# Attention of a hybrid mLSTM / windowed-attention layer: scores kept in PSUM through maximum, two exponentials and low half, outputs normalised at the end, heads spread over an iteration

## The chip, the cores and the metric

The kernel runs on one core of a Trainium2 chip. The metric is the device time of one execution in microseconds. Everything below that is a time comes from the profile of one execution of the kernel before, from its three timed runs, or from an answer of its trace.

## The reference

One layer: modulated RMS norm, one combined input projection, two token mixers side by side (a bidirectional mLSTM and windowed grouped-query attention), a gated merge, and a convolutional feed-forward. The change touches only attention of the latent tokens. Sizes: 1024 latent tokens, 256 context tokens, 16 query heads in 4 groups over 4 key heads, head size 64, window 128 in blocks of 128.

```python
def one_block(args):
    blk, qblk, kblk, vblk = args
    ...
    s_lat = jnp.einsum('btkgd,bskd->bkgts', qblk, kblk).astype(jnp.float32) * ATT_SCALE
    s_lat = jnp.where(valid, s_lat, NEG_INF)
    s_ctx = jnp.einsum('btkgd,bskd->bkgts', qblk, k_ctx).astype(jnp.float32) * ATT_SCALE
    p = jax.nn.softmax(jnp.concatenate([s_lat, s_ctx, sink_b], axis=-1), axis=-1).astype(v.dtype)
    return (jnp.einsum('bkgts,bskd->btkgd', p[..., :3 * T], vblk)
            + jnp.einsum('bkgts,bskd->btkgd', p[..., 3 * T:3 * T + C], v_ctx))
```

So each block of 128 queries of one group sees up to three key tiles of its band, two context tiles and one sink logit a head: five key tiles, or four at the two ends of the sequence.

## The kernel before

Matrix products run in fp32r, and an operand that must be exact is split in two, a high part and the rest, so that a product becomes two or three. Attention is a software pipeline over 32 pairs (g, b): group g of four heads, block b of 128 queries. Iteration n of the loop at L764 does, for different pairs at once:

- `proj` (L551): 24 products of the projected queries, key and value of pair n (tile `pq`), and from them V, the sums of squares `ss` and the rotated queries and key `qf`, on ACT, DVE and POOL;
- `stacks` (L593) for pair n-1: the key scaled and doubled (`kf`, on DVE), three transposes on TensorE (tile `qt`), then queries `QT` and keys `KA`, `KB` as high part and rest;
- `filler` (L725): 24 products of a later gate (tile `g`), which need nothing of attention and are dealt out among the others;
- `scores` (L619) for pair n-3: for each of four heads four products into a PSUM tile `s` of two banks (two such tiles), DVE's masked maximum (L645), which also copies the scaled scores to SBUF (`P`), ACT's exponential with the sum (L649); after all four heads one short chain with the sink (L653 to L657) gives four reciprocals; then for each head POOL multiplies to an f16 high half (L663), DVE makes the f16 low half (L664, `scalar_tensor_tensor`), and SP issues a DMA transpose of both halves into `T` (L665);
- `pv` (L672) for pair n-4: for each key tile ACT widens the high half of T to fp32r (`ph`) and POOL the low half (`pl`), TensorE multiplies both with V into `po`, and ACT, DVE and SP bring out `o` to DRAM.

One buffer holds T, three each hold `ph` and `pl`, six hold P. A scheduler of the language orders the program: each engine's queue is in order, and it may place an instruction ahead of one written earlier; `tc.issue_after` pins some. SP's queue carries, besides the transposes, the loads of weights (`w1r`, `fr`, `wmb`) and the stores (`sga`, `sgm`, `attT`). The modulation products (`mod_product`) put one or two sums (`macc`) a turn on DVE.

Of the kernel before, what the change touches and what calls it, by code (L numbers as in the profile page):

```python
# [36 lines left out]
PSCALE = 32768.0  # L37
# [496 lines left out]
def stage_attention(E, st, at):  # L534
# [13 lines left out]
    G = {}  # L548
    S1, S2, S3, S4 = {}, {}, {}, {}

    def proj(g, b):  # L551
        if b == 0:
# [5 lines left out]
            )  # L558
        n = f"{g}_{b}"
        ps = mm_tile(f"pq{n}")  # L560
        wn = 400 if g == 0 else 384
        mm3(nc, ps[:, :wn], hT, G[g]["w"], sl(b * P, P), sl(0, wn))
# [29 lines left out]

    def stacks(g, b):  # L593
# [3 lines left out]
        nc.vector.tensor_scalar(kf, qf[:, None, 256:320].to_broadcast([P, 2, HD]), ss[:, 4:5], None, op0=ALU.mult)  # L597


# [3 lines left out]
        nc.tensor.transpose(pt[:, 256:384], kf.rearrange("p r d -> p (r d)"), ident)  # L603
        QT = wp.tile([P, 512], F32R, tag="QT", name=f"QT{n}", bufs=3)
# [14 lines left out]
    def scores(g, b):  # L619
# [12 lines left out]
        Ps, prior = [], None  # L632
        for h in range(4):
            ps = s_tile(f"s{n}_{h}")
            q = QT[:, h * P : (h + 1) * P]
            with behind(prior):
                nc.tensor.matmul(ps[:, lat], q, KA[:, b0 * P : b1 * P], start=True, stop=False)  # L637
                nc.tensor.matmul(ps[:, lat], q, KB[:, b0 * P : b1 * P], start=False, stop=True)
                nc.tensor.matmul(ps[:, con], q, KcA[:, g], start=True, stop=False)
                last = nc.tensor.matmul(ps[:, con], q, KcB[:, g], start=False, stop=True)  # L640
            prior = FILL.products(6) if h in (0, 1, 2) else None
            pm = pp.tile([P, 960], F32, tag="P", name=f"P{n}_{h}", bufs=6)
            ex = pm[:, W // 2 : W // 2 + W]
            hh = 4 * g + h
            nc.vector.tensor_tensor_reduce(  # L645
                ex, ps[:, every], mask, scale=ss[:, h : h + 1], scalar=nsink[:, hh : hh + 1],
                op0=ALU.add, op1=ALU.min, accum_out=st4[:, h : h + 1],
            )
            nc.scalar.activation(  # L649
                ex, ex, AF.Exp, bias=st4[:, h : h + 1], scale=-1.0, accum_out=st4[:, 4 + h : 5 + h]  # L650
            )
            Ps.append((ex, pm.bitcast(F16)[:, : 2 * W].rearrange("p (a c) -> p a c", a=2)))
        nc.vector.tensor_tensor(st4[:, 8:12], st4[:, 0:4], sink[:, 4 * g : 4 * g + 4], op=ALU.add)  # L653
        nc.scalar.activation(st4[:, 8:12], st4[:, 8:12], AF.Exp)
        nc.vector.tensor_tensor(st4[:, 8:12], st4[:, 8:12], st4[:, 4:8], op=ALU.add)
        nc.vector.tensor_scalar(st4[:, 8:12], st4[:, 8:12], 1.0 / PSCALE, None, op0=ALU.mult)
        nc.vector.reciprocal(st4[:, 12:16], st4[:, 8:12])  # L657
        nk = W // P
        T = tq.tile([P, 5120], F16, tag="T", name=f"T{n}")[:, : nk * 1024].rearrange("p (a k h q) -> p a k h q", a=2, h=4, q=P)
        for h in range(4):  # L660
            ex, (hi, lo) = Ps[h][0], (Ps[h][1][:, i] for i in range(2))
            r = st4[:, 12 + h : 13 + h]
            nc.gpsimd.tensor_scalar(hi, ex, r, 1.0, op0=ALU.mult, op1=ALU.mult)  # L663
            nc.vector.scalar_tensor_tensor(lo, ex, r, hi, op0=ALU.mult, op1=ALU.subtract)  # L664
            nc.sync.dma_start_transpose(  # L665
                T.rearrange("p a k h q -> p (a k) h q")[:, :, h], Ps[h][1].rearrange("p a c -> p (a c)")
            )
# [96 lines left out]
    for n in range(N + 5):  # L764
# [3 lines left out]
        if n < N:  # L768
            proj(*seq[n])
# [1297 lines left out]
```

## Time and profile before

| | |
|---|---|
| median of 3 runs | 1987.13 us (1987.01 to 1990.43) |
| profiled execution | 1987.95 us, span 1986.1 us, granted clock 0.98 |
| attention's steady part, 148 to 696 us | 548 us |

In the profile, PE is TensorE, PEld its weight loads, DVE VectorE, ACT ScalarE, POOL GpSimd, SP the engine that issues most DMAs. A row of a group reads: line, engine, operation, output<-inputs, shapes, count, then busy us and mean ns of one, then the idle time just before them and what ended it. A row of waits reads: who waited <- for whom, us in all, times, longest. A row of the timeline reads: start, duration, engine, line, operation, count of merged instructions, and in brackets the idle time ahead of it and what ended it. In the table of windows each engine has busy time and count.

### The profile page before, as it was taken

Reading aid. Unit: us, or ns where it says so; the run is one execution under the profiler, and the core shown is the slowest. Engines: PE = TensorE matmul, PEld = TensorE weight load, DVE = VectorE, ACT = ScalarE, POOL = GpSimd, SP = SyncE. Lnnn points to the kernel's source line nnn. Section 1 sums busy time; section 2 is a strip of 40 time slices with the busy share of each in tenths; the row PEclk is TensorE's granted clock in tenths of the full one; section 3 lists DMA queues with packets and bytes.
Section 4 is the critical chain, followed back from the end, with each engine's and each line's share of the span. In section 5 each row is a group of like instructions: output and inputs, shape, how many; then the busy total and the mean of one; then the engine's idle time right before and its main releaser. Section 6 shows DMA issues by size and latency. Waiting matters only on the chain.

```text
span 1986.1 us, 27108 instructions
## 1 busy us (share of the span) xinstructions
PE 1856.4 (93%) x9029; PEld 1563.1 (79%) x9029; DVE 1513.0 (76%) x2928; ACT 982.5 (49%) x1942; POOL 440.6 (22%) x676
## 2 busy tenths in 40 slices
PE   7998888888898789999999999999999999999999
PEld 4887677677787578988788888787888888888887
DVE  3867877878888748584857788769988988997565
ACT  4635555455555525444444566347544444455441
POOL 1225555455555514030202002100000000000000
PEclk9999998899999999999999999999999999999999
DMA  9636755756666652524351994642255544489851
GB/s 350 189 110 121 151 126 118 161 115 135 151 139 131 141 156 64 178 65 158 121 168 39 368 380 151 210 156 74 106 202 194 187 170 162 177 294 335 314 181 64
DMA packets 299165, 338.17 MB, mean 170 GB/s; under 512 B 175232, under 2 KB 199696, under 8 KB 296208
## 3 DMA queue, kind: packets, MB, share of 16 engines
q1 hardware_dynamic: 284624, 310.21, 51.2%
q10 hardware_dynamic: 14400, 26.22, 4.0%
q8 instruction: 71, 1.16, 0.3%
q14 instruction: 70, 0.57, 0.1%
HBM read 220.42 MB, written 76.10 MB: 149 GB/s over the span
## 4 chain that ended last, share of the span: by engine, by line
PE 47%; DVE 3%; DMA 2%; issue 2%; ACT 2%; POOL 1%; POOLq 0%; ACTq 0%; DVEq 0%
PE pa L1645 4%; PE pa L1646 4%; PE pa L1647 4%; PE dx L1647 2%; PE dx L1645 2%; PE dx L1646 2%; PE pb L1646 2%; PE pb L1647 2%; PE pb L1645 2%; PE yb L1645 2%; PE yb L1646 2%; PE yb L1647 2%; PE dy L1647 2%; PE dy L1646 2%; PE dy L1645 2%
## 5 line engine op out<-in xcount | busy, mean ns | idle before, releaser
L664 DVE SCALAR_TENSOR_TENSOR P<-P,st 128x640 f16<-128x640 f32 (+1 forms) x128 | 151.0, 1237 | 26.5 <-POOL P L663 26.1
L663 POOL TENSOR_SCALAR P<-P,st 128x640 f16<-128x640 f32 (+1 forms) x128 | 134.0, 1062 | 76.9 <-DVE st L657 72.1
L645 DVE CUSTOM_DVE_ANT_0 P<-s,maskA,nsink 128x640 f32<-128x640 f32 (+1 forms) x128 | 113.7, 906 | 22.3 <-PE s L640 20.1
L691 POOL TENSOR_SCALAR pl<-T 128x512 fp32r<-128x512 f16 x152 | 100.9, 682 | 89.1 <-DMA T<-P 74.4
L649 ACT ACTIVATE P<-P,st 128x640 f32<-128x640 f32 (+1 forms) x128 | 101.6, 795 | 35.4 <-DVE st L645 33.0
L46 ACT ACTIVATE ph<-T 128x512 fp32r<-128x512 f16 x152 | 86.9, 619 | 59.6 <-DMA T<-P 54.0
L742 PE MATMUL g<-hH,fh 128*128 128x512 f32 x256 | 103.7, 405 | 2.2 <-ACT fo L46 2.2
L742 PE MATMUL g<-hH,fl 128*128 128x512 f32 x256 | 102.1, 399 | 0.0
L742 PE MATMUL g<-hL,fh 128*128 128x512 f32 x256 | 102.0, 398 | 0.0
L99 PE MATMUL pq<-w1l,hH 128*128 128x384 f32 (+1 forms) x256 | 89.9, 351 | 11.0 <-DVE w1l L76 11.0
L98 PE MATMUL pq<-w1h,hH 128*128 128x384 f32 (+1 forms) x256 | 89.2, 348 | 1.4 <-ACT w1h L46 1.4
L1059 POOL TENSOR_SCALAR kwh<-k,gcall 128x128 fp32r<-128x128 f32 x72 | 34.7, 486 | 248.4 <-PE dC L99 202.6
L100 PE MATMUL pq<-w1h,hL 128*128 128x384 f32 (+1 forms) x256 | 88.8, 347 | 0.0
L98 PE MATMUL kv<-w1h,hH 128*128 128x384 f32 x208 | 71.1, 343 | 4.6 <-ACT w1h L46 2.9
L99 PE MATMUL kv<-w1l,hH 128*128 128x384 f32 x208 | 71.3, 343 | 0.6 <-DVE w1l L76 0.6
L100 PE MATMUL kv<-w1h,hL 128*128 128x384 f32 x208 | 70.4, 339 | 0.0
L637 PE MATMUL s<-KA,QT 128*128 128x384 f32 (+1 forms) x128 | 47.4, 371 | 24.6 <-DVE st L645 24.5
L1783 ACT ACTIVATE cv<-ua,vecT 128x1024 f32<-128x1024 f32 x22 | 27.4, 1244 | 84.0 <-DVE ua L1756 84.0
L1645 PE MATMUL dx<-dwh,dfh 128*128 128x512 f32 (+1 forms) x176 | 68.4, 388 | 0.0
L1647 PE MATMUL dx<-dwh,dfl 128*128 128x512 f32 (+1 forms) x176 | 68.3, 388 | 0.0
L1646 PE MATMUL dx<-dwl,dfh 128*128 128x512 f32 (+1 forms) x176 | 68.2, 387 | 0.0
L683 PE MATMUL po<-ph,V 128*128 128x512 f32 x88 | 41.9, 476 | 24.2 <-ACT ph L46 23.9
(602 smaller groups left out, 6297.4 us busy)
## 6 DMA issues: line engine op xcount, KB each, us to landing
ur<-in_w_up SPq DMA_DIRECT2D x22, 1024.0 KB, 4.9
wmb<-in_w_modB SPq DMA_DIRECT2D x48, 256.0 KB, 3.0
f_d<-cv SPq DMA_DIRECT2D x22, 512.0 KB, 2.7
wm<-in_w_modA SPq DMA_DIRECT2D x16, 512.0 KB, 10.2
fr<-in_w_g SPq DMA_DIRECT2D x32, 256.0 KB, 3.0
drf<-fs_d SPq DMA_DIRECT2D x15, 512.0 KB, 7.4
drw<-wt_d SPq DMA_DIRECT2D x14, 512.0 KB, 6.5
w1b<-in_w_cx SPq DMA_DIRECT2D x16, 388.0 KB, 4.6
```

The source lines that it names most:

```text
L98: nc.tensor.matmul(ps, lh[:, ls], rh[:, rs], start=start and i == 0, stop=False)
L99: nc.tensor.matmul(ps, lh[:, ls], rl[:, rs], start=False, stop=False)
L100: nc.tensor.matmul(ps, ll[:, ls], rh[:, rs], start=False, stop=stop and i == n - 1)
L645: nc.vector.tensor_tensor_reduce(ex, ps[:, every], mask, scale=ss[:, h : h + 1], scalar=nsink[:, hh : hh + 1], op0=ALU.add, op1=ALU.min, a ...
L649: nc.scalar.activation(ex, ex, AF.Exp, bias=st4[:, h : h + 1], scale=-1.0, accum_out=st4[:, 4 + h : 5 + h])
L663: nc.gpsimd.tensor_scalar(hi, ex, r, 1.0, op0=ALU.mult, op1=ALU.mult)
L664: nc.vector.scalar_tensor_tensor(lo, ex, r, hi, op0=ALU.mult, op1=ALU.subtract)
L691: nc.gpsimd.tensor_scalar(plo, lo, 1.0 / PSCALE, 1.0, op0=ALU.mult, op1=ALU.mult)
L742: return lambda: nc.tensor.matmul(ps, w, x, start=i == 0, stop=i == len(todo) - 1)
L1645: nc.tensor.matmul(ps, lh, rh, start=start and i == 0, stop=False, skip_group_check=True)
L1646: nc.tensor.matmul(ps, lh, rl, start=False, stop=False, skip_group_check=True)
L1647: nc.tensor.matmul(ps, ll, rh, start=False, stop=stop and i == n - 1, skip_group_check=True)
```

## The change

Scores stay in the PSUM tile. DVE's masked maximum writes back to it. ACT adds a constant (15 ln 2, for the scale of the f16 halves) to the maximum, makes the f16 high half by one exponential straight from PSUM, and by a second exponential, in place in PSUM, the f32 value with the sum. DVE's low half is a `tensor_tensor` of the PSUM value and the f16 half. The transpose of a head stands directly behind its low half and no longer behind the reciprocals. The halves are not normalised: the four reciprocals of a pair are transposed to a row on TensorE (`norm_row`), go through DRAM and come back broadcast to 64 partitions (`R`), and POOL multiplies the finished output with them. POOL now widens both halves of T, by a copy, for all key tiles of a pair at the head of an iteration; `kf` is made by ACT. The loop is written so that the four heads of a pair, the 24 projection products, the 24 filler products and the ten value products alternate in fixed pieces. Buffers of T, `ph`, `pl` and `s` stay as many; P has four.

```diff
+    def norm_row(pt):
+        if not SUMS:
+            return
+        sums, j = SUMS.pop()
+        nc.tensor.transpose(pt, sums, ident)
+        row = wp.tile([4, P], F32, tag="row", name=f"row{j}", bufs=1)
+        copy_act(nc, row, pt)
+        nc.sync.dma_start(norm_d[j].rearrange("(h t) -> h t", h=4), row)
+        R[j] = wp.tile([HD, 512], F32, tag="R", name=f"R{j}", bufs=1)
+        nc.sync.dma_start(R[j], norm_d[j : j + 1].to_broadcast([HD, 512]))
...
     def stacks(g, b):
...
-        nc.vector.tensor_scalar(kf, qf[:, None, 256:320].to_broadcast([P, 2, HD]), ss[:, 4:5], None, op0=ALU.mult)
+        copy_act(nc, kf, qf[:, None, 256:320].to_broadcast([P, 2, HD]), scale=ss[:, 4:5])
...
+        norm_row(pt[0:4, 384:512])
...
+        def head(h, prior=None):
+            s = s_tile(f"s{n}_{h}")
...
+            e = s[:, every]
             hh = 4 * g + h
             nc.vector.tensor_tensor_reduce(
-                ex, ps[:, every], mask, scale=ss[:, h : h + 1], scalar=nsink[:, hh : hh + 1],
-                op0=ALU.add, op1=ALU.min, accum_out=st4[:, h : h + 1],
+                e, e, mask, scale=ss[:, h : h + 1], scalar=nsink[:, hh : hh + 1],
+                op0=ALU.add, op1=ALU.min, accum_out=st4[:, 8 + h : 9 + h],
             )
-            nc.scalar.activation(
-                ex, ex, AF.Exp, bias=st4[:, h : h + 1], scale=-1.0, accum_out=st4[:, 4 + h : 5 + h]
-            )
...
-        for h in range(4):
-            ex, (hi, lo) = Ps[h][0], (Ps[h][1][:, i] for i in range(2))
-            r = st4[:, 12 + h : 13 + h]
-            nc.gpsimd.tensor_scalar(hi, ex, r, 1.0, op0=ALU.mult, op1=ALU.mult)
-            nc.vector.scalar_tensor_tensor(lo, ex, r, hi, op0=ALU.mult, op1=ALU.subtract)
-            nc.sync.dma_start_transpose(
-                T.rearrange("p a k h q -> p (a k) h q")[:, :, h], Ps[h][1].rearrange("p a c -> p (a c)")
-            )
+            m = st4[:, h : h + 1]
+            nc.scalar.activation(m, st4[:, 8 + h : 9 + h], AF.Identity, bias=shift)
+            two = pp.tile([P, 1280], F16, tag="P", name=f"P{n}_{h}", bufs=4)
+            hi, lo = two[:, :W], two[:, W : 2 * W]
+            nc.scalar.activation(hi, e, AF.Exp, bias=m, scale=-1.0)
+            nc.scalar.activation(e, e, AF.Exp, bias=m, scale=-1.0, accum_out=st4[:, 4 + h : 5 + h])
+            nc.vector.tensor_tensor(lo, e, hi, op=ALU.subtract)
+            nc.sync.dma_start_transpose(T[:, :, h], two[:, : 2 * W])
...
-            copy_act(nc, ph, hi, scale=1.0 / PSCALE)
-            nc.gpsimd.tensor_scalar(plo, lo, 1.0 / PSCALE, 1.0, op0=ALU.mult, op1=ALU.mult)
+            for i, x in enumerate((ph, plo)):
+                nc.gpsimd.tensor_copy(x, T[:, i * nk + kb].rearrange("p h q -> p (h q)"))
...
+        def end():
+            o2 = wp.tile([HD, 512], F32, tag="o2", name=f"o2{n}", bufs=1)
+            copy_act(nc, o2, po[HD:P])
+            nc.vector.tensor_tensor(o2, po[0:HD], o2, op=ALU.add)
+            nc.gpsimd.tensor_tensor(o2, o2, R.pop(g * NB + b), op=ALU.mult)
...
     for n in range(N + 5):
...
+        if head:
+            head(0)
+        if turned:
+            stacks(*turned)
+        elif SUMS:
+            norm_row(tp_tile(f"nr{n}")[0:4, :P])
+        last = new.some(17)
+        if head:
+            head(1, last)
+        new.some(7)
+        if now:
+            projected(*now, ps)
+        last = FILL.some(6)
+        if head:
+            head(2, last)
+        FILL.some(9)
+        last = old.some(4)
+        if head:
+            head(3, last)
+            sums()
+        for k in (2, 2, 2):
+            FILL.some(3)
+            old.some(k)
+        if end:
+            end()
```

How the scheduled queues move is shown at three places, all in the iteration that scores group 1, block 3 (`P1_3_0` to `P1_3_3` are its heads). First ACT, around the last exponentials of the block. Before:

```order
L46 ACTIVATE ph1_2_1_3472<-T1_2_3269 128x512
L649 ACTIVATE P1_3_0_3410,st1_3_3398<-P1_3_0_3410,st1_3_3398 128x640
L649 ACTIVATE P1_3_1_3424,st1_3_3398<-P1_3_1_3424,st1_3_3398 128x640
L649 ACTIVATE P1_3_2_3438,st1_3_3398<-P1_3_2_3438,st1_3_3398 128x640
L46 ACTIVATE ph1_2_2_3476<-T1_2_3269 128x512
L46 ACTIVATE ph1_2_3_3482<-T1_2_3269 128x512
L649 ACTIVATE P1_3_3_3446,st1_3_3398<-P1_3_3_3446,st1_3_3398 128x640
L654 ACTIVATE st1_3_3398<-st1_3_3398 128x4
L46 ACTIVATE ph1_2_4_3488<-T1_2_3269 128x512
L46 ACTIVATE fo6_0_3508<-g6_0_3397 128x512
```

The change:

```order
L688 ACTIVATE st1_3_3449<-st1_3_3449,shift_1111 128x1
L691 ACTIVATE P1_3_2_3570<-s1_3_2_3563,st1_3_3449 128x640
L692 ACTIVATE s1_3_2_3563,st1_3_3449<-s1_3_2_3563,st1_3_3449 128x640
L46 ACTIVATE kf1_6_3670<-qf1_6_3548,ss1_6_3543 128x128
L46 ACTIVATE fo6_0_3624<-g6_0_3447 128x512
L688 ACTIVATE st1_3_3449<-st1_3_3449,shift_1111 128x1
L46 ACTIVATE o21_2_3619<-po1_2_3451 64x512
L691 ACTIVATE P1_3_3_3595<-s1_3_3_3588,st1_3_3449 128x640
L692 ACTIVATE s1_3_3_3588,st1_3_3449<-s1_3_3_3588,st1_3_3449 128x640
L698 ACTIVATE st1_3_3449<-st1_3_3449 128x4
```

The widening copies `ph` are gone from between the exponentials; `kf`, `fo` and `o2` of other pairs now stand between those of the third head and those of the fourth.

Second POOL, around the copies of T for the pair before (`T1_2`). Before:

```order
L573 TENSOR_TENSOR ss1_6_3358<-ss1_6_3358,expo_62 128x5
L574 TENSOR_SCALAR ss1_6_3358<-ss1_6_3358 128x4
L590 TENSOR_TENSOR qf1_6_3363<-qf1_6_3363,t21_6_3364 128x320
L691 TENSOR_SCALAR pl1_2_0_3469<-T1_2_3269 128x512
L691 TENSOR_SCALAR pl1_2_1_3473<-T1_2_3269 128x512
L691 TENSOR_SCALAR pl1_2_2_3477<-T1_2_3269 128x512
L691 TENSOR_SCALAR pl1_2_3_3483<-T1_2_3269 128x512
L691 TENSOR_SCALAR pl1_2_4_3489<-T1_2_3269 128x512
L663 TENSOR_SCALAR P1_3_0_3410<-P1_3_0_3410,st1_3_3398 128x640
```

The change:

```order
L718 CAST pl1_2_2_3461<-T1_2_3255 128x512
L600 TENSOR_SCALAR ss1_6_3543<-ss1_6_3543 128x5
L718 CAST ph1_2_3_3464<-T1_2_3255 128x512
L718 CAST pl1_2_3_3465<-T1_2_3255 128x512
L718 CAST ph1_2_4_3468<-T1_2_3255 128x512
L718 CAST pl1_2_4_3469<-T1_2_3255 128x512
L601 TENSOR_TENSOR ss1_6_3543<-ss1_6_3543,expo_62 128x5
L602 TENSOR_SCALAR ss1_6_3543<-ss1_6_3543 128x4
L618 TENSOR_TENSOR qf1_6_3548<-qf1_6_3548,t21_6_3549 128x320
L728 TENSOR_TENSOR o21_2_3619<-o21_2_3619,R10_3494 64x512
L718 CAST ph1_3_0_3638<-T1_3_3450 128x512
```

`qf` of pair (1, 6), which `kf1_6` above reads, stood ahead of the copies of T and now stands behind all ten of them.

Third SP. Before:

```order
L756 DMA sga_d_66<-fo6_0_3508 128x512
L665 DMA_TRANSPOSE T1_3_3454<-P1_3_0_3410 128x10x128
L665 DMA_TRANSPOSE T1_3_3454<-P1_3_1_3424 128x10x128
L665 DMA_TRANSPOSE T1_3_3454<-P1_3_2_3438 128x10x128
L665 DMA_TRANSPOSE T1_3_3454<-P1_3_3_3446 128x10x128
L700 DMA attT_d_64<-o21_2_3504 64x4x128
```

The change:

```order
L628 DMA norm_d_1110<-row10_3491 4x128
L221 DMA wmb22_3628<-in_w_modB 128x512
L750 DMA fr7_1_3830<-in_w_g 128x512
L73 DMA w1r33_3835<-in_w_att 128x2x384
L630 DMA R10_3494<-norm_d_1110 64x512
L694 DMA_TRANSPOSE T1_3_3450<-P1_3_0_3479 128x10x128
L694 DMA_TRANSPOSE T1_3_3450<-P1_3_1_3527 128x10x128
L694 DMA_TRANSPOSE T1_3_3450<-P1_3_2_3570 128x10x128
L772 DMA sga_d_66<-fo6_0_3624 128x512
L221 DMA wmb23_3631<-in_w_modB 128x512
L729 DMA attT_d_64<-o21_2_3619 64x4x128
L694 DMA_TRANSPOSE T1_3_3450<-P1_3_3_3595 128x10x128
```

The two DMAs of the reciprocals stand ahead of the block's first transpose, and a store, a load and the output of the pair before stand ahead of its last.

More of the change, by code (lines that the diff above doesn't have):

```diff
@@ L36 @@
 EPS = 1e-6
-PSCALE = 32768.0
+PSHIFT = 15.0 * math.log(2.0)
 NEG = -1e30
@@ L672, in pv @@
+        return head, sums
     def pv(g, b):
@@ L749, in filled @@
             return
-        FILL.products(len(FILL.todo))
+        FILL.some(len(FILL.todo))
         c, t, ps = FILL.tile
@@ L767, in stage_attention @@
             done += 1
[L768 to L771 removed]
+        now, turned, scored, valued = (seq[n - d] if 0 <= n - d < N else None for d in (0, 1, 3, 4))
         if n not in SKIPS and n < N + len(SKIPS):
[L773 to L777 removed]
+            filler(n - sum(k < n for k in SKIPS))
+        ps, new = proj(*now) if now else (None, Products())
+        head, sums = scores(*scored) if scored else (None, None)
+        old, end = pv(*valued) if valued else (Products(), None)
+        if head:
[23 more added lines that the diff above has]
+            end()
         filled()
```

114 lines of the change are left out of this document (50 added, 64 removed).

## The prediction

> **What bounds the kernel now.** I read the windows first, to see where TensorE is not busy, then who made it wait there, then one iteration in order of time. In a window the pairs are busy time (and instructions) of PE, PEld, DVE, ACT and POOL, then come the granted clock and the DMA share.
>
> ```profile
> 148.00:696.00 548.00, 463.33 (x2249) 389.03 (x2248) 445.76 (x963) 291.28 (x669) 297.72 (x386) 0.95 0.63 135
> 696.00:712.00 16.00, 9.30 (x36) 7.68 (x35) 2.07 (x4) 4.10 (x8) 6.86 (x39) 0.73 0.74 174
> ```
>
> Attention's steady part is 548 us, with PE idle for 84.7 of it and no other engine near full: DVE is at 81%, POOL at 54%, ACT at 53%. So work waits for work. TensorE's waits in this stage (us in all, times, longest):
>
> ```profile
> PE po L683 <- ACT ph L46: 31.4, 27, 7.2
> PE s L637 <- DVE st L645: 24.5, 16, 3.2
> PE po L684 <- POOL pl L691: 12.7, 8, 3.0
> PE pq L99 <- DVE w1l L76: 7.8, 3, 4.7
> ```
>
> The first and third are the value products waiting for widened pieces of T. The pieces wait for the transposes, and one iteration shows why these come late:
>
> ```profile
> 478.58 1.51 SPq L665 DMA_TRANSPOSE T<-P  x1
> ...
> 482.30 1.67 ACT L46 ACTIVATE ph<-T 128x512 fp32r<-128x512 f16 x3 [1.45 <-DMA T<-P]
> ...
> 486.55 0.81 ACT L649 ACTIVATE P<-P,st 128x640 f32<-128x640 f32 x1
> ...
> 487.98 0.18 DVE L657 RECIPROCAL st<-st 128x4 f32<-128x4 f32 x1
> ...
> 488.33 4.25 POOL L663 TENSOR_SCALAR P<-P,st 128x640 f16<-128x640 f32 x4 [2.13 <-DVE st L657]
> ...
> 489.17 4.89 DVE L664 SCALAR_TENSOR_TENSOR P<-P,st 128x640 f16<-128x640 f32 x4 [1.01 <-POOL P L663]
> ...
> 490.61 6.46 SPq L665 DMA_TRANSPOSE T<-P  x4
> ```
>
> It is a ring: transposes land, ACT widens among its exponentials, the fourth exponential ends, one reciprocal releases all four heads, POOL and DVE make halves for 5 us, SP issues four transposes. All four heads wait for the last. The ring's turn is the period:
>
> ```profile
> 148.33 1.35 SPq L665 DMA_TRANSPOSE T<-P  x1
> ...
> 696.43 1.26 SPq L665 DMA_TRANSPOSE T<-P  x1
> ...
> 708.01 0.34 PE L98 MATMUL kv<-w1h,hH 128*128 128x384 f32 x1
> ```
>
> The first two are the first transposes of the first and of the 32nd block: 548.1/31 = **17.68 us** an iteration. PE's own work in it is 463.3/31 = 14.95 us. That is the most the change can reach while the clock stays as it is.
>
> **The change part by part.** Prices now (busy us, mean ns of one, idle before):
>
> ```profile
> L664 DVE SCALAR_TENSOR_TENSOR P<-P,st 128x640 f16<-128x640 f32 x96 | 118.4, 1291 | 20.1 <-POOL P L663 19.9
> L663 POOL TENSOR_SCALAR P<-P,st 128x640 f16<-128x640 f32 x96 | 104.7, 1106 | 59.7 <-DVE st L657 54.9 <-ACT fo L46 2.8 <-ACT ph L46 1.9
> L691 POOL TENSOR_SCALAR pl<-T 128x512 fp32r<-128x512 f16 x150 | 99.7, 683 | 89.0 <-DMA T<-P 74.4 <-PE po L684 11.7 <-PE s L640 2.1
> L645 DVE CUSTOM_DVE_ANT_0 P<-s,maskA,nsink 128x640 f32<-128x640 f32 x96 | 88.5, 939 | 16.8 <-PE s L640 16.4
> L46 ACT ACTIVATE ph<-T 128x512 fp32r<-128x512 f16 x151 | 86.4, 619 | 59.6 <-DMA T<-P 54.0 <-issue 5.4 <-PE po L683 0.2
> L649 ACT ACTIVATE P<-P,st 128x640 f32<-128x640 f32 x96 | 78.7, 821 | 28.2 <-DVE st L645 27.0 <-issue 0.8 <-DVE st L657 0.2
> L573 POOL TENSOR_TENSOR ss<-ss,expo 128x5 f32<-128x5 f32 x32 | 38.0, 1187 | 2.5
> L590 POOL TENSOR_TENSOR qf<-qf,t 128x320 f32<-128x320 f32 x32 | 27.9, 870 | 0.0
> L699 DVE TENSOR_TENSOR o<-po,o 64x512 f32<-64x512 f32 x31 | 20.9, 676 | 5.3 <-ACT o L46 5.3
> L46 ACT ACTIVATE fo<-g 128x512 f32<-128x512 f32 x32 | 18.7, 586 | 13.5 <-PE g L742 13.5
> L46 ACT ACTIVATE o<-po 64x512 f32<-64x512 f32 x31 | 18.4, 595 | 29.9 <-PE po L684 29.4
> L597 DVE TENSOR_SCALAR kf<-qf,ss 128x128 f32<-128x128 f32 x32 | 12.4, 388 | 17.5 <-POOL qf L590 17.5
> L46 ACT ACTIVATE KA<-qt 128x128 fp32r<-128x128 f32 x32 | 8.8, 276 | 0.3
> L572 POOL TENSOR_SCALAR ss<-ss 128x5 f32<-128x5 f32 x29 | 6.1, 210 | 100.0 <-DVE ss L571 99.6
> L654 ACT ACTIVATE st<-st 128x4 f32<-128x4 f32 x32 | 6.1, 191 | 1.3 <-DVE st L653 1.3
> L1400 POOL TENSOR_TENSOR sgm<-sgm,y 128x512 f32<-128x512 f32 x8 | 11.9, 1496 | 134.7 <-DMA wo0r<-in_w_o 104.7 <-issue 24.0 <-ACT bmah L46 3.4
> ```
>
> *The low half.* It becomes a subtraction of an SBUF operand from a PSUM one. The trace's nearest row is o<-po,o (L699): 676 for 512 elements, so 0.85 for 640. L645, the other PSUM reader, gives 0.94; no gain at all is 1.29. I take 0.85. It saves 4 x 0.44 = 1.8 us of DVE an iteration; with kf gone to ACT (0.39), DVE falls from 14.4 busy (445.8/31) to about 12.2.
>
> The Trainium skill speaks against keeping scores in PSUM (Perfetto Trace Analysis, "Optimizing Scalar/DVE Operations"): DVE's fixed access cost is some 60 ns on SBUF and some 125 ns on PSUM. By that rule the low half of one head would be 0.07 us dearer than an SBUF one and the forecast 2 us later; L699's 676 ns already holds whatever PSUM costs here.
>
> *The second exponential.* ACT gains, a head, one narrow instruction (0.19, like L654) and one exponential into f16 without a sum: between 0.62 (ph, 512 wide) and 0.82 (L649), I take 0.75. Four heads cost 3.8, kf 0.28, the row 0.28. It loses five ph copies, 3.1. ACT goes from 9.4 (291.3/31) to 10.6 us: not a bound by itself.
>
> *POOL.* It loses four high halves (4.4) and gains five more copies of T (ten in all) and the final product. For a copy I take the 0.62 of ph; the bounds are that and pl's mean of 0.68, which is 0.6 us a turn, and an f16 copy of POOL's own kind is not in the trace at this size. The product is 64x512 with two inputs: 1.5 by L1400. The sum is 9.6 - 4.4 + 3.1 + 1.5 = 9.8 us.
>
> *The row of reciprocals*: a transpose on PE, a copy on ACT, two small DMAs on SP. The result is needed only after the last value product, most of an iteration later, and that hides it; uncovered it would be two landings, each as long as a transpose's below, 7 us. It adds three waits. On PE the transpose waits for the reciprocal, and the rest of the projection is queued behind it: in the order its place varies from directly behind the first head to some 20 projection products later, and where it stands early I expect up to half a microsecond of PE idle, inside the slack of 16.2 - 14.95. On SP the second DMA waits for the landing of the first, and the next block's transposes are queued behind; T is not yet free then. On POOL the final product waits for DVE's sum, and the next block's first copy is queued behind; that one waits for the transposes anyway, which land later.
>
> *The spread heads.* Each head's transpose is issued right behind its low half. No head waits for the reciprocal, and only the last head is on the ring. What is late next is read from the order: on ACT, kf for a later block stands ahead of the last head's exponentials (in some iterations fo and o2 as well); kf waits for POOL's qf, and POOL does that behind nearly all of its ten copies. Those wait for the last transpose of the block before. So there is a new ring:
>
> ```profile
> L665 SPq DMA_TRANSPOSE T<-P x128: 1249/1464/2414, 148.3 to 700.5; - x128
> ...
> DMA to landing us min/median/max: 3.1/3.6/5.8
> ```
>
> last low half 0.85, transpose to landing 3.6, ten copies 6.2, three ss steps 0.21 + 1.19 + 0.21 = 1.6, qf 0.87, kf 0.28, narrow add 0.19, exponentials 0.75 + 0.82, and four changes of engine at 0.17 (488.33 less the end of L657 at 488.16) = 0.7: **15.9 us**. What cuts in: SP's other issues ahead of the last transpose, fo and o2 (0.59 + 0.60) in about a third of the iterations, weight splits on ACT. Call it 0.7 a turn, an estimate: 16.6. The eight blocks at the ends of the sequence have four key tiles instead of five: two copies and a fifth of the wide operations less, 1.5, so 15.1. Mean (24 x 16.6 + 8 x 15.1)/32 = 16.2.
>
> A second ring comes to nearly the same. T is one buffer: after its tenth copy come four transposes, 3 x 1.46 + 3.6 = 8.0 us, then ten copies, 6.2, with the ss steps of 1.6 among them: 15.8. And PE's own 14.95 is close behind, so I expect little slack and no turn much under 16.
>
> *Sum.* 31 x (17.68 - 16.2) = 46 us. The drain (696.4 to the next stage's first product at 708.0) I leave as it is: the transposes end sooner there, but eight copies stand on one engine. The profiled execution took 1987.95 (span 1986.1 and 1.85 around it), 0.8 over the median of the three runs, so the result is **1942 us** from the profiled time and 1941 from the median; the 0.8 is far inside the range and I write 1942.
>
> **Rivals.** *PE becomes the bound.* Queues slide past each other, the rings keep slack, and the period is 14.95: 31 x 2.73 = 85 us less, 1903. For it: both rings rest on median latencies, and stalls also slow PE down:
>
> ```profile
> 360.00:370.00 10.00, 4.11 (x16) 3.50 (x15) 9.24 (x12) 4.07 (x8) 4.32 (x4) 0.66 1.06 240
> 370.00:380.00 10.00, 9.12 (x32) 7.25 (x31) 5.02 (x16) 4.89 (x10) 6.13 (x9) 0.66 0.50 148
> ```
>
> Behind the 4.7 us wait for w1l the granted clock is 0.66 for 20 us; at clock 1 the 463 us of PE would be 463 x 0.95 = 440, which puts the low end at 1987 - 108 = 1880. Against it: two rings within 1 us above it.
> The Trainium skill (TensorE: Matmul & The Clock Gate, "What's actually happening") halves the clock only after an idle window of some 3.4 us; by it the 1880 needs no PE without waits, just none that long, and the trace agrees as far as this 4.7 us wait goes.
>
> *A wait for the score banks takes the old one's place.* There are two score tiles; a head's must now live through maximum, both exponentials and the low half: 0.94 + 0.19 + 0.75 + 0.82 + 0.85 + 0.7 = 4.3 us, instead of 0.94. Between head h and h+2 lie some 34 matmuls of 463.33/2249 = 0.206, 7.0 us. That hides it until the queues of ACT and DVE add 2.7. If they do in two heads of four by half a microsecond more, the period is 17.2 and the time 31 x 0.48 = 15 less, 1973.
>
> *Slower.* The new ring runs through four engines that serve in order; if it exceeds 17.68 the change loses. That takes 1.5 us more than my 16.2: copies of 0.77, or landings of 5.1 (the longest is 5.8) because transposes now run among other transfers, or DVE late with q's products, which delays qf and so kf and with it the exponentials behind. At 18.3 it is +19, 2007.
>
> *Nothing moves*: the two rings are equal, 1987.
>
> **How the numbers follow.** Chances: forecast (15.7 to 16.9 a turn, 1925 to 1963) 0.47; PE bound 0.18; score banks 0.12; slower 0.17; nothing 0.06. About 0.2%, 4 us, is what a measurement here can tell from no change. Faster 0.77, same 0.06, slower 0.17. Range 1893 to 1992: it leaves out most of the slower case and the clock's full recovery.
>
> **What would show it.** Right: 30 to 32 first transposes 16 to 16.6 us apart; PE waits for ph gone; ACT's largest wait is kf for POOL's qf, late in an iteration; POOL's first copy waits for the transposes; low half under 0.95. Wrong: PE at 97% of the stage (first rival), PE's s waiting for the low half (second), copies well over 0.7 or periods over 17.7 (third). A low half at 1.29 or an exponential from PSUM over 1 us would break the prices themselves.

## The result, and the profile after

The changed kernel takes 1970.93 us (median of four runs, 1965.22 to 1971.98). The kernel before, run beside it on the same chip, takes 1988.03. The ratio is 0.9906, with a 95% interval of 0.9885 to 0.9928: faster by 0.9%, 17 us, where 46 were forecast. The profiled execution of after took 1965.22 us, with a span of 1963.2.

The windows of after, with the columns explained ahead of the prediction's first fence: attention's steady part, and the drain behind it.

```profile
139.00:671.00 532.00, 472.04 (x2339) 391.54 (x2337) 378.72 (x921) 340.90 (x846) 290.68 (x442) 0.98 0.64 149
671.00:690.00 19.00, 10.54 (x37) 8.51 (x37) 5.29 (x10) 2.64 (x9) 11.60 (x43) 0.64 0.71 179
```

TensorE is idle for 60 of 532 us, where it was 84.7 of 548. DVE has shed 67 us and ACT has gained 50. The marks that the prediction used, the first transpose of the first block, that of the 32nd, and the first product of the next stage, are these rows of the timeline:

```profile
139.98 3.13 SPq L694 DMA_TRANSPOSE T<-P  x2
...
671.34 6.88 SPq L694 DMA_TRANSPOSE T<-P  x4
...
682.35 0.52 PE L98 MATMUL kv<-w1h,hH 128*128 128x384 f32 x1
```

The period is (671.34 - 139.98)/31 = 17.14 us, against 17.68 before and 16.2 forecast. The two spans differ by 22.9 us, and all of it can be placed: 8.35 at the start (the first transpose comes at 139.98 and not 148.33: the first exponential starts 2.0 earlier, at 137.66 and not 139.64, and a head then no longer waits for the other three), 16.7 in the 31 turns, 0.6 in the drain (11.0 against 11.6), and 2.8 given back in the stages behind. That the 16.7 of the turns equals the 17 of the medians is chance: the profiled execution of after is the fastest of its four.

The waits of after from 130 to 690 us, in the form of the prediction's:

```profile
POOL ph L718 <- DMA T<-P: 106.2, 29, 7.3
ACT kf L46 <- POOL qf L618: 76.2, 28, 5.3
...
POOL ss L600 <- DVE ss L599: 30.6, 12, 9.1
...
PE po L722 <- POOL ph L718: 19.9, 11, 6.8
PE qt L625 <- DVE st L700: 15.9, 14, 2.2
```

POOL waits for the transposes, ACT waits with kf for POOL's qf: that is the ring that the prediction drew. One turn shows both rings. The rows are the timeline's of POOL, ACT, SP and again POOL, in order of time within an engine:

```profile
473.13 0.61 POOL L718 CAST ph<-T 128x512 fp32r<-128x512 f16 x1 [3.75 <-DMA T<-P]
...
481.76 0.61 POOL L718 CAST pl<-T 128x512 fp32r<-128x512 f16 x1
482.34 0.87 POOL L618 TENSOR_TENSOR qf<-qf,t 128x320 f32<-128x320 f32 x1
...
483.24 0.40 ACT L46 ACTIVATE kf<-qf,ss 128x128 f32<-128x128 f32 x1 [2.71 <-POOL qf L618]
483.55 0.77 ACT L691 ACTIVATE P<-s,st 128x640 f16<-128x640 f32 x1
...
482.40 2.80 SPq L694 DMA_TRANSPOSE T<-P  x2
485.31 1.01 SPq L750 DMA_DIRECT2D fr<-in_w_g  x2
486.37 2.13 SPq L694 DMA_TRANSPOSE T<-P  x1
488.59 0.53 SPq L772 DMA_DIRECT2D sgm_d<-fo  x1
489.21 0.38 SPq L221 DMA_DIRECT2D wmb<-in_w_modB  x1
489.64 2.61 SPq L694 DMA_TRANSPOSE T<-P  x1
...
494.95 0.61 POOL L718 CAST ph<-T 128x512 fp32r<-128x512 f16 x1 [3.82 <-DMA T<-P]
```

The tenth copy ends at 482.37, and the next block's first transpose is issued at 482.40: it waited for T. Between the first transpose and the last, 7.24 us apart, SP issues two loads of fr, a store and a load of wmb. This is the longest turn, 21.8 us. The table for the mean turn is made from the single records of these instructions in the trace (a row of the timeline merges neighbours), for the third block's turn to the 28th's (26 turns, first copies from 186.78 to 634.96). "After" and "two T" (an experiment below) are means in us; 6 of the 26 blocks have four key tiles, while the predicted pieces are for five. Some expectations below carry 6.12, 3.78 and 4.14 for the 6.09, 3.81 and 4.10 of this table.

| piece of a turn | as predicted | after | two T |
|---|---|---|---|
| first copy to the end of the tenth, ss steps among them | 6.2 + 1.6 | 7.31 | 7.33 |
| tenth copy's end to the first transpose's issue | 0 | 0.03 | -6.90 |
| first transpose's issue to the last one's | 3 x 1.46 = 4.38 | 6.09 | |
| last transpose's issue to the next first copy | 3.6 | 3.81 | 3.68 |
| **the ring through T: their sum** | **15.8** | **17.24** | |
| tenth copy's end to the end of qf | 0.87 | 1.54 | 1.56 |
| to the end of kf | 0.28 + 0.17 | 0.48 | 0.48 |
| to the last transpose's issue | 0.19 + 0.75 + 0.82 + 0.85 + 0.5 | 4.10 | 3.73 |
| **the ring through qf and kf, with copies and landing** | **15.9, with extras 16.6** | **17.24** | **16.78** |

Both sums close by construction; which ring sets the turn is for the experiments. In all 31 turns of after the first transpose goes out 0.03 us after the last copy of the block before. The prices of single instructions:

```profile
L718 POOL CAST pl<-T 128x512 fp32r<-128x512 f16 x152 | 100.5, 661 | 0.0
L718 POOL CAST ph<-T 128x512 fp32r<-128x512 f16 x152 | 97.6, 642 | 118.4 <-DMA T<-P 106.2 <-DMA norm_d<-row 7.6 <-PE s L680 4.1
L693 DVE TENSOR_TENSOR P<-s,P 128x640 f16<-128x640 f32 x96 | 78.6, 820 | 38.6 <-ACT s L692 38.2
L691 ACT ACTIVATE P<-s,st 128x640 f16<-128x640 f32 x96 | 75.9, 791 | 1.8
L728 POOL TENSOR_TENSOR o<-o,R 64x512 f32<-64x512 f32 x32 | 42.8, 1339 | 105.1 <-DVE st L700 74.3 <-DVE o L727 22.0 <-DVE st L697 5.0
L688 ACT ACTIVATE st<-st,shift 128x1 f32<-128x1 f32 x128 | 37.1, 290 | 59.0 <-DVE st L683 53.5 <-DVE gtile L592 4.8
L46 ACT ACTIVATE kf<-qf,ss 128x128 f32<-128x128 f32 x32 | 12.9, 402 | 81.5 <-POOL qf L618 78.0 <-POOL ss L601 3.5
```

### The profile page after: what moved, and what is told of

It reads as the page before. It is cut to its first block, busy times and chain, and to the rows that moved or that the text cites. A ratio compares the mean times of both kernels' runs of the same rounds, so it can differ in the third digit from the quotient of the medians.

```text
span 1963.2 us, 27633 instructions
## 1 busy us (share of the span) xinstructions
PE 1856.4 (95%) x9061; PEld 1555.9 (79%) x9061; DVE 1440.9 (73%) x2864; ACT 1029.5 (52%) x2110; POOL 434.1 (22%) x733
## 4 chain that ended last, share of the span: by engine, by line
PE 56%; DMA 12%; POOL 10%; DVE 8%; ACT 7%; issue 6%; SPq 0%; ACTq 0%; POOLq 0%; DVEq 0%
PE pa L1682 4%; PE pa L1683 4%; PE pa L1684 4%; DMA T<-P 4%; POOL pl L718 3%; POOL ph L718 3%; PE dx L1684 2%; PE dx L1682 2%; PE dx L1683 2%; PE pb L1683 2%; PE pb L1682 2%; PE pb L1684 2%; PE kv L99 2%; PE kv L98 2%; PE kv L100 2%
## 5 line engine op out<-in xcount | busy, mean ns | idle before, releaser
L693 DVE TENSOR_TENSOR P<-s,P 128x640 f16<-128x640 f32 (+1 forms) x128 | 100.6, 787 | 53.1 <-ACT s L692 52.7
L683 DVE CUSTOM_DVE_ANT_0 s<-s,maskA,nsink 128x640 f32<-128x640 f32 (+1 forms) x128 | 116.3, 909 | 24.0 <-PE s L680 23.3
L718 POOL CAST ph<-T 128x512 fp32r<-128x512 f16 x152 | 97.6, 642 | 118.4 <-DMA T<-P 106.2
L718 POOL CAST pl<-T 128x512 fp32r<-128x512 f16 x152 | 100.5, 661 | 0.0
L691 ACT ACTIVATE P<-s,st 128x640 f16<-128x640 f32 (+1 forms) x128 | 97.9, 765 | 3.2 <-DMA T<-P 0.5
L692 ACT ACTIVATE s<-s,st 128x640 f32<-128x640 f32 (+1 forms) x128 | 94.1, 736 | 0.0
L688 ACT ACTIVATE st<-st,shift 128x1 f32<-128x1 f32 x128 | 37.1, 290 | 59.0 <-DVE st L683 53.5
L728 POOL TENSOR_TENSOR o<-o,R 64x512 f32<-64x512 f32 x32 | 42.8, 1339 | 105.1 <-DVE st L700 74.3
```

Of the source, the lines that this page charges most:

```text
L683: nc.vector.tensor_tensor_reduce(e, e, mask, scale=ss[:, h : h + 1], scalar=nsink[:, hh : hh + 1], op0=ALU.add, op1=ALU.min, accum_out=st4 ...
L691: nc.scalar.activation(hi, e, AF.Exp, bias=m, scale=-1.0)
L693: nc.vector.tensor_tensor(lo, e, hi, op=ALU.subtract)
L718: nc.gpsimd.tensor_copy(x, T[:, i * nk + kb].rearrange("p h q -> p (h q)"))
```

## The experiments

Each kernel is after with the edit shown. The ratios are to the kernel before as it ran in the same group on the same chip, with the 95% interval; 0.01 is 20 us.

| run | kf | qf | T | other | us | ratio to before |
|---|---|---|---|---|---|---|
| after | ACT | POOL | 1 | | 1970.9 | 0.9906 (0.9885 to 0.9928) |
| e1 | DVE | POOL | 1 | | 1957.4 | 0.9871 (0.985 to 0.9892) |
| e3 | ACT | DVE | 1 | | 1963.2 | 0.9892 (0.9876 to 0.9908) |
| e12 | DVE | DVE | 1 | | 1956.9 | 0.9847 (0.9825 to 0.9869) |
| e2 | ACT | POOL | 2 | | 1936.7 | 0.9761 (0.9743 to 0.978) |
| e8 | DVE | POOL | 2 | | 1919.9 | 0.9669 (0.9637 to 0.9701) |
| e4 | DVE | DVE | 2 | | 1907.3 | **0.9611** (0.9592 to 0.9629) |
| e7 | ACT | POOL | 1 | ph on ACT | 1952.8 | 0.9847 (0.9825 to 0.9868) |
| e11 | DVE | DVE | 2 | ph on ACT | 1940.2 | 0.9762 (0.9729 to 0.9796) |
| e6 | ACT | POOL | 1 | not spread | 1990.2 | 1.0016 (0.9997 to 1.0036) |
| e10 | DVE | DVE | 2 | not spread | 1968.7 | 0.9914 (0.9889 to 0.9939) |
| e5 | ACT | POOL | 1 | fr, sg on ACT's queue | 1981.2 | 0.9984 (0.9967 to 1.0001) |
| e9 | ACT | POOL | 1 | not normalised | 1958.5 | 0.9855 (0.9839 to 0.987) |

**Which ring: kf, qf and T.** The edits of e1, e2 and e3 (e4, e8 and e12 combine them):

```diff
-        copy_act(nc, kf, qf[:, None, 256:320].to_broadcast([P, 2, HD]), scale=ss[:, 4:5])
+        nc.vector.tensor_scalar(kf, qf[:, None, 256:320].to_broadcast([P, 2, HD]), ss[:, 4:5], None, op0=ALU.mult)
...
-    tq = st.enter_context(tc.tile_pool(name="att", bufs=1, reuse_waits="tile"))
+    tq = st.enter_context(tc.tile_pool(name="att", bufs=2, reuse_waits="tile"))
...
-        nc.gpsimd.tensor_tensor(qf, qf, t2, op=ALU.add)
+        nc.vector.tensor_tensor(qf, qf, t2, op=ALU.add)
```

kf on DVE:

> kf (the scaled copy of q's last column block) goes back from ACT to DVE; nothing else. In the trace of after a turn lasts 17.24 us on the mean of 26 turns: first copy to tenth copy's end 7.31, to the end of qf 1.53, to the end of kf 0.48, to the issue of the last transpose 4.14, to the first copy of the next block 3.78. Theory (the ring through kf): with kf off ACT, the third and fourth heads' exponentials no longer stand behind qf, and what is left is the ring of the one T buffer with its transposes back to back: 7.31 + 3 x 1.46 + 3.78 = 15.5 us, near TensorE's own 472.04/31 = 15.2; 31 x (17.14 - 15.5) = 51 us less, about 1920, between 1912 and 1945. Rival 1 (the T buffer alone sets the turn, whatever stands behind kf): no gain, 1962 to 1975. Rival 2 (TensorE's own scattered waits): no gain either.

It came out at 1957.4, between the two ranges, a gain of 0.0035 on after (7 us) with intervals that overlap. The wait that was to go did go, and the time hardly followed. In e1 from 130 to 690 us, ACT's wait for qf is no longer listed; DVE has it, and POOL waits for the transposes as before:

```profile
POOL ph L718 <- DMA T<-P: 109.5, 26, 7.1
...
DVE kf L636 <- POOL qf L618: 29.3, 17, 3.8
```

The first transposes are still issued 0.03 us after the last copies, and the turn is 17.06 on the mean of the same 26. So the ring through kf was not the one that set the turn.

Two T:

> T has two buffers in place of one; nothing else. Theory (the ring through kf): the first two transposes of a block may go before the tenth copy, but the last one still stands behind qf, kf and the exponentials, so the turn stays within half a us of 17.1: 1955 to 1972. Rival 1 (the T buffer sets the turn: every first transpose is issued 0.02 to 0.03 us after the tenth copy ends): the turn falls to TensorE's 15.2 to 15.6, 48 to 60 us less, 1911 to 1925. Rival 2 (TensorE's own waits): no gain.

1936.7: a gain of 0.0145 on after, 29 us, four times that of e1, and yet between the two theories. Both were half right. The last column of the table is this run: the first transposes now go out 6.90 us ahead of the end of the last copy, so T's ring is gone; what is left is the other ring, at 16.78, and here ACT's wait in it has grown from 76.2 to 90.8 us:

```profile
ACT kf L46 <- POOL qf L618: 90.8, 28, 6.9
...
POOL ph L718 <- DMA T<-P: 52.9, 17, 6.9
```

qf on DVE:

> The add that makes qf (30.8 us over 32 on POOL) goes to DVE; nothing else. qf, and with it kf, no longer stands behind the ten copies on POOL. Theory (the ring through kf): left is the ring of T, 15.5 us: about 1922, between 1912 and 1945; ACT's wait of 76.2 us for qf mostly goes. Rival 1 (T buffer alone): no gain but POOL's 0.96 us of qf, which stood behind the last copy and not in that ring: 1962 to 1975. Rival 3 (DVE, busy 378.72 of 532 us, becomes the bound when 0.6 to 1 us an iteration is added): slower than after, above 1975.

1963.2, in the range of the T buffer alone, and not told apart from after. POOL's wait for the transposes grew from 106.2 to 137.8 us: qf left POOL, POOL came to its next wait sooner. The turn stayed: 17.38 on the mean, with the first transposes still 0.03 us behind the last copies. T's ring alone held it. The same says e12, both edits with one T:

> kf and qf on DVE, with one T buffer as in after. Theory (T's ring alone: copies and ss steps 7.1, first to last transpose 5.3 with SP's other issues, landing 3.8): a turn of 16.2 us, 31 x (17.14 - 16.2) = 29 us less than after: about 1942, between 1933 and 1955. Rival (the ring through qf and kf was the costly one, as each of the two edits alone left a part of it): 1908 to 1925, as with two T buffers.

1956.9, a little above the expected stretch. Its turn is 17.24 on the mean, as in after, although nothing stands behind qf any more: 6.8 for the copies, 6.49 from the first transpose to the last, 3.9 to the next first copy. Of the 6.49, three transposes take 4.43, other issues of SP between them 1.09, and for 0.97 SP issues nothing. In after the same split of 6.09 is 4.28, 0.93 and 0.88. So the stretch is not made by kf. Its larger part is SP's queue, which holds everything back while T is not free and then serves it in order; of the time in which SP issues nothing, some 0.3 us a turn are gaps of less than 0.15 us between two issues, and the rest are waits in 8 of the 26 turns of e12 and in 13 of after.

With both rings cut:

> kf on DVE, qf on DVE and two T buffers together: both rings are cut. Theory (the two rings): the turn comes down to TensorE's own work, 15.2 to 15.6 us, 31 x (17.14 - 15.4) = 54 us less than after: about 1917, between 1910 and 1935, and little below the kernels with one ring cut (1920). Rival 2 (TensorE's scattered waits, 60 us in the 31 iterations, for reciprocals, score banks and copies of P, each for its own reason): the turn stays near 17 and the time above 1955.

1907.3, 3.9% below the kernel before and inside the expected range. Its windows, and what TensorE still waits for from 140 to 625 us (the first three rows):

```profile
137.00:626.00 489.00, 464.85 (x2341) 388.25 (x2340) 403.92 (x983) 335.84 (x822) 270.53 (x415) 0.99 0.75 163
...
PE po L722 <- POOL ph L718: 7.2, 7, 2.0
PE qt L625 <- DVE st L700: 2.5, 7, 0.7
PE s L677 <- DVE V L595: 2.0, 2, 1.7
```

TensorE is busy for 95% of this part. The mean turn is 15.65, or 15.43 by the marks (138.18 to 616.60). With T doubled and only kf moved:

> kf on DVE and two T buffers, with qf left on POOL behind the copies. Two T buffers alone gave 1936.7, with qf on DVE besides 1907.3. Theory (with T doubled, what is left is qf -> kf -> the exponentials queued behind kf on ACT): kf on DVE takes ACT's wait of 90.8 us away and gives most of the 29 us: 1908 to 1920. Rival (it is qf's place behind the ten copies, whoever makes kf: the stacks, the next scores and PE wait for it): 1928 to 1938.

1919.9, at the upper edge of the theory's range: kf gives 18 us of the 30 between e2 and e4 by the ratios, qf the other 12. (The profiled execution of e8, at 1909.95 its fastest, has a turn of 15.74, so the traces do not show where qf's 12 us lie.) Here both matter, and with one T neither did: the edits do not add up, because the ring that they shorten is only the longer one when T is doubled. This is also why the forecast for e1 failed.

**The copies of the high half back on ACT.**

```diff
-                nc.gpsimd.tensor_copy(x, T[:, i * nk + kb].rearrange("p h q -> p (h q)"))
+                src = T[:, i * nk + kb].rearrange("p h q -> p (h q)")
+                if i == 0:
+                    copy_act(nc, x, src)
+                else:
+                    nc.gpsimd.tensor_copy(x, src)
```

> The five copies of the high half (ph) go back to ACT, as before the change; POOL keeps the five of the low half. Theory (the T buffer's ring: copies 7.31 with the three short steps on ss, 6.12 between transposes, 3.78 landing): the copies run side by side and the first part falls by about 3 us; the turn is then TensorE's, 15.2 to 15.8: about 1920, between 1912 and 1938. Rival (ACT takes over as the bound of the ring: its copies wait in its queue for the transposes to land, as POOL's did for 106.2 us, and the next heads' exponentials stand behind them): above 1955.

1952.8, between the two. T's ring stays closed: the first transposes still go out 0.03 to 0.09 us after the last copy in 29 of 31 turns. The turn is 16.84, and its copies take 5.82 of it, where the theory had some 3 us less than 7.31. ACT's rows show why:

```profile
586.14 1.67 ACT L46 ACTIVATE ph<-T 128x512 fp32r<-128x512 f16 x3
...
592.68 1.14 ACT L46 ACTIVATE ph<-T 128x512 fp32r<-128x512 f16 x2
```

Here three copies use up the three buffers of ph, and the last two come 4.9 us later, behind exponentials. With the rings cut by other means, only that price is left:

> e4 (kf and qf on DVE, two T buffers) with the copies of the high half on ACT besides. Theory (after e4 TensorE sets the turn: 464.85 busy of 489.00 us in its stretch): at most the 24 us of waits are left to win, and the copies are off the turn by now: within 6 us of e4, 1901 to 1914. Rival (the copies on POOL still set the turn of 15.65 us): 1890 to 1898. Rival (ACT's queue, with its copies waiting for transposes ahead of exponentials, becomes a bound): above 1918.

1940.2, 30 us worse than e4, as the last rival had it. TensorE's waits in e11, from 140 to 640 us, against those of e4 above:

```profile
PE po L726 <- ACT ph L46: 18.6, 14, 3.3
PE s L677 <- DVE P L693: 12.0, 15, 2.4
```

So it is better to have all ten copies on POOL once T and qf no longer wait for POOL, and dearer while they do.

**The order of the iteration.** e6 takes the loop back to the order before, all else as after; e10 does the same to e4:

```diff
-        if head:
-            head(0)
...
+        if now:
+            ps, new = proj(*now)
+            new.some(24)
+            projected(*now, ps)
...
+            for h in range(4):
+                head(h, last)
+                last = FILL.some(6) if h < 3 else None
+            sums()
...
+            old.some(len(old.todo) - 2)
+            old.some(2, FILL.some(6))
+            end()
```

> The iteration's order is put back as it was before the change (products of the projection in one piece, the four heads with six products of the filler behind each of the first three, the product with V at the end); the rest as after. Theory (the rings through T, the copies and kf set the turn, not TensorE's order): the turn keeps 16.8 to 17.7 us, so 1960 to 1990, within 20 us of after. Rival (the spread is what the gain comes from, the rest only makes it possible): the turn goes back above 17.7 and the time above 1990.

1990.2, with a ratio whose interval holds 1. The turn is 18.37, and 18.13 by the marks, above before's 17.68, as the rival had it (though 1990.2 lies on the border of the two ranges): without the spread, the rest of the change gains nothing that can be measured. Here 7.44 us lie between the first transpose and the last, with 1.84 us of SP's other issues between them.

> The iteration's order as before the change (as in e6), with kf and qf on DVE and two T buffers (as in e4). With one T buffer the spread was worth 19 us (1990.2 against 1970.9); in the trace of e6 the stretch from a block's first to its last transpose was 7.42 us, against 6.12. Theory (the spread gains by shortening that stretch inside T's ring, so nothing is left for it once T is doubled): within 8 us of e4, 1900 to 1916. Rival (the spread gains on TensorE, whose waits for scores and for the last copies it fills, whatever T does): 15 us or more above e4, 1922 and up.

1968.7, 60 us above e4. The theory said that the spread works only inside T's ring, and it falls: with the rings cut the spread is worth 60 us, nearly three times the 22 that it is worth in after by the ratios of e6. The waits of e10 from 130 to 690 us show where:

```profile
DVE s L683 <- PE s L680: 89.0, 62, 5.7
...
PE po L722 <- POOL ph L718: 35.1, 31, 3.2
```

In e4 the same two are 25.9 (27 times) and 9.3 (8 times). With the old order DVE waits for scores that TensorE has not come to, and TensorE later waits for copies: the spread is a gain of TensorE's order itself.

**SP's other issues.**

```diff
-                nc.sync.dma_start(raw, A["w_g"][c][:, 4 * i : 4 * i + 4, :])
+                nc.scalar.dma_start(raw, A["w_g"][c][:, 4 * i : 4 * i + 4, :])
...
-        nc.sync.dma_start(dst[(c % 8) * P : (c % 8 + 1) * P, t * 512 : (t + 1) * 512], o)
+        nc.scalar.dma_start(dst[(c % 8) * P : (c % 8 + 1) * P, t * 512 : (t + 1) * 512], o)
```

> The two loads of fr and the store of sg of an iteration are issued from ACT's queue in place of SP's; everything else as after. In the trace of after 6.12 us pass on the mean between the issue of a block's first and last transpose, where three transposes take 4.4; 0.93 us of it is other issues of SP (fr, sg, wmb, attT) that stand between. Theory (the one T buffer's ring sets the turn, and what SP issues inside it counts in full): some 0.5 us of the 0.93 goes, 31 x 0.5 = 15 us less than after: about 1955, between 1945 and 1963. Rival (the last transpose waits for its head anyway, behind kf, so SP's order costs nothing): within 5 us of after, 1966 to 1976. Rival (a load issued by ACT waits there for its buffer, with the exponentials behind it): slower than after, above 1976.

1981.2: slower than after, above the last rival's bound. The other issues between the transposes fell from 0.93 to 0.59 us a turn, the stretch only to 5.99, and the last transpose's issue to the next first copy went from 3.81 to 4.63; the turn is 17.57. So the transposes came in later. The Trainium skill (Trainium Kernel Development and Optimization, "Key Constraints") says that transfers from the queues of SP, ACT and POOL run on the same DMA engines and that a second queue only saves issue time; the trace agrees on the second half, with 0.34 us of SP's issues saved. That loads on the same DMA engines cost the 0.82 us of later landing is likely but not shown: in e6, with no loads on ACT, the same piece takes 4.36. Whether ACT's waits in its own queue add to it is not told apart, and what the 0.93 us would be worth by themselves stays open.

**The row of reciprocals.** e9 leaves out the row's transposes, its two transfers and the final product, so its attention is not normalised.

> Left out, on top of after: the normalisation at the end (the transposes of the reciprocals, the row's two transfers, and POOL's product with R), so the outputs of the attention stay unnormalised. Theory (the T buffer's ring sets the turn): the row's transpose and the final product lie outside it, except that POOL's product and SP's three issues stand where copies and transposes wait: 0 to 0.5 us a turn, 1955 to 1972. Rival (TensorE's 15.9 us of waits for the reciprocals, 14 of them, are paid in full, with 1.34 us of POOL's product a turn): 16 to 45 us less, 1925 to 1955.

1958.5, 10 us below after by the ratios and inside what the theory allowed. TensorE's 15.9 us of waits for the reciprocals are gone, and its wait for ph has grown from 8.6 to 17.0 us in the window from 140 to 640. POOL waits for the transposes for 243.5 us instead of 106.2; in after it stood 101 us ahead of the final product (74.3, 22.0 and 5.0), which is left out here:

```profile
POOL ph L712 <- DMA T<-P: 243.5, 30, 11.6
...
PE po L716 <- POOL ph L712: 17.0, 14, 3.3
```

Waits were removed, and about half of TensorE's and all of POOL's came back under another name, as long as the ring held.

## Why the prediction was right and wrong

*The sign, the ring's way and most prices were right.* The low half costs 0.82 (0.85 taken), the f16 exponential 0.79 (0.75), copies 0.64 and 0.66 (0.62, with 0.68 as bound), the final product 1.34 (1.5). Too low were the narrow add, 0.29 for 0.19, and kf, 0.40 for 0.28. The chain from copies to qf, kf, exponentials and the last transpose is there as drawn, and ACT's largest wait is kf's. TensorE's waits for ph shrank from 31.4 us to 19.9, of which 6.8 is one wait in the drain, but did not go. On the low half, the Trainium skill's rule (Perfetto Trace Analysis, "Optimizing Scalar/DVE Operations") was 0.07 us a head for a PSUM operand. The trace does not show such a price: at 128x512 this subtraction with its PSUM operand takes 687 ns, and the subtraction of two SBUF operands at L51 takes 755, though that one writes a wider type.

```profile
L693 DVE TENSOR_TENSOR P<-s,P 128x512 f16<-128x512 f32 x32 | 22.0, 687 | 14.5 <-ACT s L692 14.5
...
L51 DVE TENSOR_TENSOR fl<-fr,fh 128x512 fp32r<-128x512 f32 x30 | 22.7, 755 | 0.8 <-ACT fh L46 0.8
```

*The step that failed is the second ring: "four transposes, 3 x 1.46 + 3.6 = 8.0 us".* The mechanism was named, T is one buffer, but the term of three transposes was taken from the kernel before, where all four go out in one piece (6.46 us for four, in the prediction's rows). In after the stretch measures 6.09, not 4.38: the three transposes themselves are no dearer (4.28), but 0.93 goes to SP's other issues and 0.88 is time in which SP issues nothing, gaps and heads that were not ready. The prediction did count what cuts in, 0.7 us a turn, and it counted it in the first ring alone. In the 20 turns with five key tiles the ring's pieces are 7.50 for the copies (7.8 taken), 6.07 and 3.79 (3.6 taken), so this term is the one that is far off. With 1.71 more, the ring that was to come "to nearly the same" is the longer one, at 17.24, and the gain of 46 us shrinks to the 16.7 that the turns brought.

The run with T doubled confirms it: it lies 47 us below before by its ratio, close to the forecast, and its turn is 16.44 by the marks, against 16.2 forecast. That the 47 meets the 46 is partly luck, since 38 of it come from the turns and most of the rest from the start, which was not in the sum.

*The first ring was also too short, by less.* With T doubled it shows itself at 16.78, against 16.6 with the 0.7 for what cuts in. Against the bare sum it is longer in qf, 1.56 instead of 0.87, as some of POOL's short steps fall behind the last copy (in 15 of these 26 turns) when the first of them waits for DVE's sum (30.7 us, 16 times, in that run), a part of what the rival "slower" described; and between kf and the last transpose, 3.73 instead of 3.1.

*The rivals.* The wait for score banks did not come: TensorE waited 8.6 us in all for the low half to free a bank. TensorE as the bound was not the outcome, but e4 shows that its price was near: 15.43 a turn by the marks with the rings cut, against the 14.95 given as the most. *The drain*, left as it was, moved by 0.6. *The row*: half a microsecond of TensorE a turn was expected and 15.9/31 = 0.51 came; "inside the slack" was less sure, since leaving out the row and the final product gains 10 us. *The start* was not in the sum at all, and 8.35 us came from there. *The spread* was priced only as heads that no longer wait for the reciprocal; by e6 the rest of the change gains nothing without it.

## What to carry to other kernels

When a change turns one burst of transfers into several issues spread over an iteration, price the stretch from first to last as the issuing queue will serve it, with everything that stands between, and do so for every ring that runs through it. When two rings lie within a microsecond of each other, taking a wait out of one shows little; cut both in one experiment before judging either (here kf alone gave 7 us and T alone 29, and with qf they gave 59 together). And look for the single buffer: the first transfer issued 0.03 us after the last reader in every turn shows it, and doubling it was one number in the code.

## What was not expected of the hardware

Of the 304 copies on POOL in after, 285 take about 0.61 us and 19 take 0.85 to 1.36; together the 19 cost 10 us. Each of the 19 overlaps an instruction of DVE that reads two operands from SBUF (the weights' low halves at L76 and L51, the accumulation at L236). For example, POOL's row and DVE's:

```profile
473.69 1.35 POOL L718 CAST pl<-T 128x512 fp32r<-128x512 f16 x1
...
473.54 1.02 DVE L76 TENSOR_TENSOR w1l<-w1r,w1h 128x768 fp32r<-128x768 f32 x1
474.48 0.81 DVE L693 TENSOR_TENSOR P<-s,P 128x640 f16<-128x640 f32 x1
```

The copy ends at 475.04, 0.48 us after DVE's L76 does. In all 19 DVE had started first. Where POOL starts first, in 24 other overlaps, the copy keeps its 0.61 us and DVE's instruction can be the longer one, 1.37 us at most. (In one more, DVE starts 0.02 us first and the copy still keeps its time.) The new low half (L693) has one operand in PSUM, and 95 of the copies that keep their 0.61 us overlap one. The Trainium skill (SBUF — State Buffer, "SBUF: two separate sides") gives the reason as a lock: a GpSimd instruction and a DVE instruction with two SBUF inputs share one pair of ports, and whichever starts first has it for the whole instruction. The rows agree.

The trace of before shows the same for the pair that the change took away. Of POOL's 96 high halves of 640 elements (L663), 54 began while a DVE instruction with two SBUF operands was running, mostly the low half of another head, and took 1.36 us (median); the other 42 took 0.80. DVE's low half (L664) took 0.87 us in the 21 cases without a POOL instruction beside it and 1.41 to 1.42 in the 72 where POOL had started first. So its mean of 1291 ns was in good part a wait for POOL. The 0.85 that the prediction took from a row with a PSUM operand was right, but the saving of some 0.47 us comes mainly from no longer waiting for POOL, which the prediction did not name.

The granted clock was 0.98 in the steady part of after and 0.64 in the drain, where TensorE waits 6.83 us for one copy:

```profile
680.64 0.80 PE L722 MATMUL po<-ph,Vc 128*128 128x512 f32 x1 [6.83 <-POOL ph L718]
```

But it falls behind much shorter waits as well. One of TensorE's waits in the steady part, and the window that begins 0.6 us behind it, with half the clock:

```profile
559.94 0.27 PE L625 MATMUL qt<-ident,st 128*4 128x128 f32 x1 [2.16 <-DVE st L700]
...
560.50:563.90 3.40, 3.40 (x13) 3.40 (x12) 1.76 (x5) 2.69 (x8) 1.06 (x2) 0.51 0.99 258
```

From 140 to 640 us there are four such stretches of 3.4 us (from 188.5, 560.5, 587.8 and 628.8), and each begins within 1.1 us of the end of a wait of 1.22 to 2.39 us. In before, the clock of 0.66 that the prediction read begins at 363.2, half a microsecond into the wait of 4.70 that ends at 367.41, and not behind it. So the trace does not bear out the prediction's remark that only waits of such a length matter; what it costs is small in after, where 0.98 is left.
